# Hybrid encoder layer: the down projection product by product, gathered biases, values split once, a scheduler with a port shared by VectorE and GpSimd

## Chip, cores and metric

The kernel runs on one core of a Trainium2 chip. Its time is the device time of one execution in microseconds, the median of three runs. The core has a tensor engine (TensorE, PE in the profile; PEld are its weight loads), VectorE (DVE), ScalarE (ACT), GpSimd (POOL) and SyncE (SP), whose queue issues all DMAs here.

## The reference

One encoder layer of width 1024 on two sequences, p with 512 tokens and s with 1024, all in float32:

```python
mod = silu(c) @ w_ada + b_ada                       # sh1, sc1, g1, sh2, sc2, g2
n = rms_norm(x, ln1_g) * (1 + sc1) + sh1
q, k, v, xl, gl = split(n @ w_in)                   # 8 heads of 64; 512 columns for the recurrence
att = neighbourhood_attention(rms_norm(q), rms_norm(k), v, rpb)
xl = depthwise_conv(xl, 4 taps)
h = rg_lru(xl, forward) + rg_lru(xl, backward)
x = x + g1 * (concat([att, h * gelu(gl)]) @ w_out)
n2 = rms_norm(x, ln2_g) * (1 + sc2) + sh2
ug, uv = split(depthwise_conv(n2 @ w_up, 3 taps))   # 2816 each
x = x + g2 * ((gelu(ug) * uv) @ w_down)
```

Attention is on a grid 64 tokens wide: each token sees 8 rows by 16 columns around it, with a bias `rpb[head, row distance, column distance]` added to its scores before the softmax.

## The kernel before

**Precision.** Each float32 operand of a large product is split into a high part, rounded to TensorE's float32r, and a low part, the difference (`split`: a copy on ScalarE or VectorE, a subtraction on VectorE or GpSimd). A product is three matmuls: high by high, high by low, low by high (`mm3`).

**Strassen.** Feed-forward up and down are multiplied in Winograd's form of Strassen's scheme: seven products of half-size blocks in place of eight, with sums s1 to s4 of blocks of the left operand and t1 to t4 of the right one. The tuple `WINO` has their order, the PSUM bank in which each accumulates and whether it is the first there.

**Stages.** First the modulation and the first norm. Then the projections, attention and recurrence for four pairs of heads of p and four of s: the attention of one pair is recorded in turns with the projections of the next (`weave`). Then the output projection and the second norm, the up projection over 22 hidden tiles of 128 (four of them for p first, then the rest for both, then these four for s), with the convolution, GeLU and product done as tiles come, their results written to `g_d` in HBM. Last the down projection, from `g_d` and `w_down`.

**Down before (lines 1431 to 1534).** The 22 hidden tiles go in five chunks (`CHUNKS` = 2, 4, 6, 6 tiles, and the four of `ONLY_P`). In each chunk the loop goes over six pairs of token tiles; for each pair it loads four blocks of `g_d`, makes s1 to s4 and the parts of seven terms, and runs the seven products, each over the chunk's one to three pairs of hidden tiles. At the end of each product its bank is emptied: copies of products 1, 5 and 6, additions in the banks, and `add`, which takes the finished block into an accumulator in SBUF, or in the last chunk through the gate and the residual to the output. So every pair of token tiles is visited five times, and the banks are emptied in every visit. Terms of `w_down` are made once in a chunk (`wd_term`).

**Attention before (lines 1023 to 1105).** A query tile is 8 rows by 16 columns. Its bias is made on the chip for each head: a mask from HBM, turned to bfloat16 and kept for the sequence (`masks`), less a window of a table of the pair of heads, by an instruction on VectorE or GpSimd (line 1070). The scores have the wrong sign (the query's scale is -0.125), so that the softmax's maximum is a minimum. `qkv` writes the values to HBM in float32 (line 922 and 925); `values` loads them for each block of 16 query columns, 32 key columns wide, and splits them there (lines 1053 to 1055).

**Order.** The whole program is recorded and then put in order by a list scheduler (`run`, `_order`) that knows a cost for each instruction, the latest start that keeps TensorE going, and the memory. An instruction can have alternatives on another engine: `either=True` is ScalarE or VectorE, `pool=None` VectorE or GpSimd. `leave` decides whether the other engine would be done first, against this one's cost times a factor of the table `LEAN`. VectorE and GpSimd are planned as independent. Since one helper line emits all instructions, all have line L351 in the profile; tiles are named by the memory in which they lie (`arena_f`, `arena_r`, `piece0F`, ..., `bank` for PSUM). Two arenas divide 216 KiB a partition: F for plain data, R for parts of operands, with the share of R by stage in `STEPS` (`turn`).

Of the kernel before, what the change touches and what calls it, by code (L numbers as in the profile page):

```python
# [18 lines left out]
P = 128  # L19
D = 1024  # L20
KT = 8
# [6 lines left out]
TAB_R = 16  # L28
TAB_C = 48
# [9 lines left out]
LEAN = {("DVE", "POOL"): 0.389, ("DVE", "DVE"): 0.536, ("ACT", "ACT"): 0.611, ("ACT", "DVE"): 1.869, ("DVE", "ACT"): 1.004}  # L39
# from the end of one instruction to the start of one that waits for it  # L40
# [6 lines left out]
# products of Strassen's scheme in Winograd's form, in the order they run: name, terms of A and B, bank, first in its bank  # L47
# [3 lines left out]
CHUNKS = (2, 4, 6, 6)  # L51
# [4 lines left out]
class View:  # L56
    """A window of a buffer that has no address yet: the access pattern on a stand-in, and how to get it."""
# [32 lines left out]
    def span(self):  # L90
        """Partition range and byte range in the buffer that it can touch."""
# [43 lines left out]
class Piece:  # L135
    """Memory that belongs to one of two arenas at a time; plan holds (position in the program, arena) of each change."""
# [8 lines left out]
class Arena:  # L145
    """Memory in which buffers get their place when their first instruction is put in order."""
# [61 lines left out]
class Op:  # L208
    __slots__ = ("pos", "eng", "cost", "lat", "emit", "deps", "left", "users", "ready", "bufs", "aset", "start", "end", "vt", "done", "name", "alts", "all", "win", "ver", "key", "first", "move", "late", "strict")


class Recorder:
# [55 lines left out]
    def turn(self, step):  # L268
        """From here in the program the float32r arena has this much memory."""
# [6 lines left out]
    # buffers  # L276
# [21 lines left out]
    def pair(self, shape, name):  # L298
        """High and low parts of an operand; they get their places together."""
# [14 lines left out]
    # instructions  # L314
    def op(self, eng, cost, emit, reads, writes, aset=None, lat=0.0, also=(), alts=(), move=0.0):
# [3 lines left out]
        o.all = {eng: (cost, emit), **dict(alts)}  # L319
        o.first = eng  # L320
# [43 lines left out]
    def act(self, out, in_, func, scale=None, bias=None, accum_out=None, either=False):  # L364
# [8 lines left out]
        self.op("ACT", cost, self._emit(self.nc.scalar.activation, kw), [in_, scale, bias], [out, accum_out], aset=SETS.get(func), alts=alts)  # L373
# [8 lines left out]
    def vec(self, name, out, reads, per=1.045, base=67.0, alts=(), **kw):  # L382
# [4 lines left out]
        self.op("DVE", per * n + base + (60 if ps else 0), self._emit(getattr(self.nc.vector, name), kw), reads, w, alts=alts)  # L387
# [12 lines left out]
    def tt(self, out, in0, in1, op, pool=False):  # L400
        """On VectorE, on GpSimd (pool), or on whichever is free first (pool=None)."""
# [6 lines left out]
        else:  # L408
            self.op("DVE", *b, [in0, in1], [out], alts={"POOL": a} if pool is None else {})
# [4 lines left out]
    def mm(self, out, lhsT, rhs, start, stop, tile_position=None, also=(), cost=None, go_on=False):  # L414
        n = self._n(rhs)
        if cost is None:
            cost = max(64.0, n) / 2.4 + 2.5 if rhs.ap.dtype == F32R else max(214.0, n / 0.6)
# [6 lines left out]
        if start:  # L424
            # a group's first product clears the flags of the whole bank
# [13 lines left out]
    def mm3_rows(self, outs, sts, mvs):  # L439
        """outs[i] = sts[i].T @ mvs[i], each i on rows of the array of its own, side by side"""  # L440
# [15 lines left out]
    def mm2_rows(self, outs, sts, mvs):  # L456
        """outs[i] = sts[i][0].T @ mvs[i][0] + sts[i][1].T @ mvs[i][1], the second on rows of the array of its own"""
# [43 lines left out]
        # when each has to start for the tensor engine to go through the program without a halt  # L501
# [45 lines left out]
    def _order(self, occ):  # L547
        """The instructions and changes of memory in order, or where it halts and for which memory."""
# [20 lines left out]
        moved = 0.0  # L569
# [63 lines left out]
        while count < n:  # L633
# [69 lines left out]
            o.cost, emit = o.all[e]  # L703
            o.start, o.end = s, s + o.cost
# [38 lines left out]
def encoder(ctx: ExitStack, tc: tile.TileContext, x_p, x_s, c_t, ada, bada, lng, w_qkv, w_xg,  # L743
            qkg, tab, mask, lruv, gatew, w_out, w_up, w_down, ffv, y_p, y_s):
# [881 lines left out]
```

## Time and profile before

| | |
|---|---|
| median of three runs | 1893.22 us (1892.41 to 1893.79) |
| span of the profiled execution | 1892.9 us; its own time beside the span is not given, and the runs lie within 1 us of it |
| mean granted TensorE clock | 0.964 |
| TensorE busy | 1721.7 us, 91% |
| VectorE busy | 1495.2 us, 79% |
| ScalarE busy | 951.8 us, 50% |
| GpSimd busy | 838.9 us, 44% |
| moved by DMA | 201.12 MB, mean 106 GB/s |

Busy time is the time in which at least one instruction of the engine ran, waits inside an instruction included. Matmuls are pipelined and their ends modelled, so TensorE's share is read by stage and beside its clock. The granted clock has two levels, 1.2 and 2.4 GHz; 0.964 is their mean as a share of the upper one. Stages by time: modulation and start to 100 us; projections, attention and recurrence to 663; output projection to about 757; second norm and first up tiles to about 900; up to 1400, its end and the start of down to 1497; down to the end.

### The profile page before, as it was taken

The numbers are of one execution on the slowest core, as the hardware profiler recorded it, in microseconds if no ns is written. First come the engines' busy times: TensorE is split into PE (matmuls) and PEld (weight loads), VectorE is DVE, ScalarE is ACT, GpSimd is POOL, SyncE is SP. The second block draws the span as 40 slices with busy tenths as digits, with TensorE's granted clock in tenths as the row PEclk, the third lists the DMA queues.
The fourth block names the chain that finished last, engine by engine and source line by source line (L and its number), as shares of the span: only waits on it lengthen the run. The fifth ranks groups of instructions, "written<-read, shape, count | busy, mean of one in ns | idle before, by whom it ended". The sixth has DMA issues, their size and how long they took to land. (4 is left out here: it accounts for less than half of the span.)

```text
span 1892.9 us, 26075 instructions
## 1 busy us (share of the span) xinstructions
PE 1721.7 (91%) x8906; PEld 1416.1 (75%) x8906; DVE 1495.2 (79%) x2662; ACT 951.8 (50%) x1753; POOL 838.9 (44%) x656
## 2 busy tenths in 40 slices
PE   6987979989898899897999999999999888888978
PEld 3665767768687578797888888888887666776756
DVE  5697797897969874868767767667698998789998
ACT  3365863857676741454444444444454554243332
POOL 0364332362616321334333333333255776467874
PEclk9998989999999899998999999999999999999989
DMA  9435314040406465462122221221232331324322
GB/s 369 162 101 150 123 45 134 17 163 13 167 12 189 99 195 173 139 206 79 56 71 64 62 68 62 62 73 56 66 97 81 115 106 55 95 71 143 118 97 97
DMA packets 144695, 201.12 MB, mean 106 GB/s; under 512 B 15793, under 2 KB 83505, under 8 KB 144561
## 3 DMA queue, kind: packets, MB, share of 16 engines
q1 hardware_dynamic: 144560, 199.44, 33.2%
q8 instruction: 70, 1.15, 0.3%
q14 instruction: 65, 0.52, 0.1%
HBM read 157.97 MB, written 41.44 MB: 105 GB/s over the span
## 5 line engine op out<-in xcount | busy, mean ns | idle before, releaser
L351 PE MATMUL bank<-arena_r 128*128 128x512 f32 (+3 forms) x3487 | 859.6, 379 | 58.0 <-ACT piece0F L351 11.0
L351 PEld LDWEIGHTS bank<-arena_r 128*128 128x128 f32 (+1 forms) x3487 | 632.2, 192 | 192.3 <-issue 22.0
L351 PE MATMUL bank<-arena_r,piece0R 128*128 128x512 f32 (+3 forms) x1323 | 325.2, 346 | 8.5 <-DVE piece4F L351 4.4
L351 PEld LDWEIGHTS bank<-arena_r,piece0R 128*128 128x128 f32 (+1 forms) x1323 | 230.6, 194 | 41.5 <-issue 6.3
L351 POOL TENSOR_TENSOR arena_r<-arena_f,arena_r 128x256 fp32r<-128x256 f32 (+4 forms) x172 | 189.8, 1113 | 159.1 <-ACT arena_r L351 74.1
L351 POOL TENSOR_TENSOR arena_f<-arena_f 128x512 f32<-128x512 f32 (+5 forms) x149 | 178.9, 1207 | 99.6 <-issue 42.9
L351 ACT ACTIVATE arena_r<-arena_f 128x256 fp32r<-128x256 f32 (+4 forms) x245 | 115.0, 495 | 130.8 <-PE bank L351 77.8
L351 PE MATMUL bank<-arena_r,piece2R 128*128 128x512 f32 (+1 forms) x735 | 179.5, 335 | 0.0
L351 DVE SCALAR_TENSOR_TENSOR arena_f<-bank,arena_s,arena_f 128x255 f32<-128x255 f32 (+2 forms) x308 | 157.5, 535 | 21.2 <-ACT arena_f L351 10.5
L351 ACT ACTIVATE arena_f<-arena_f,arena_s 128x384 f32<-128x384 f32 (+2 forms) x166 | 101.7, 619 | 84.7 <-DVE arena_s L351 54.4
L351 PEld LDWEIGHTS bank<-arena_r,piece2R 128*128 128x128 f32 x735 | 126.6, 190 | 16.4 <-POOL piece2R L351 0.2
L351 PE MATMUL bank<-arena_r,piece4R 128*128 128x256 f32 (+1 forms) x453 | 137.5, 330 | 0.4 <-DVE arena_f L351 0.4
L351 DVE TENSOR_TENSOR arena_f<-arena_f 128x512 f32<-128x512 f32 (+5 forms) x148 | 134.8, 919 | 3.7 <-ACT arena_f L351 2.5
L351 DVE TENSOR_TENSOR arena_r<-arena_f,arena_r 128x256 fp32r<-128x256 f32 (+5 forms) x143 | 123.8, 882 | 6.6 <-ACT arena_r L351 2.6
L351 ACT ACTIVATE arena_f<-bank 128x512 f32<-128x512 f32 (+3 forms) x186 | 82.3, 454 | 75.1 <-DVE bank L351 36.9
L351 PE MATMUL bank<-piece0R,arena_r 128*128 128x512 f32 (+3 forms) x316 | 104.4, 398 | 2.1 <-DVE arena_s L351 2.0
L351 ACT ACTIVATE piece0R<-arena_f 128x512 fp32r<-128x512 f32 (+2 forms) x78 | 48.9, 627 | 113.1 <-PE bank L351 92.5
L351 ACT ACTIVATE arena_f<-bank,arena_s 128x512 f32<-128x512 f32 (+1 forms) x132 | 89.6, 683 | 24.5 <-PE bank L351 15.2
L351 DVE TENSOR_TENSOR bank<-bank,arena_f 128x512 f32<-128x512 f32 (+1 forms) x89 | 52.3, 589 | 51.3 <-PE bank L351 32.8
L351 PEld LDWEIGHTS bank<-arena_r,piece4R 128*128 128x128 f32 x453 | 83.5, 190 | 9.3 <-issue 0.8
L351 ACT ACTIVATE piece2R<-arena_f 128x512 fp32r<-128x512 f32 x63 | 39.8, 631 | 89.9 <-PE bank L351 77.9
L351 DVE SCALAR_TENSOR_TENSOR arena_f<-arena_f,arena_s 128x511 f32<-128x511 f32 (+3 forms) x102 | 70.9, 696 | 17.4 <-ACT arena_f L351 15.4
(432 smaller groups left out, 3214.1 us busy)
## 6 DMA issues: line engine op xcount, KB each, us to landing
arena_f<-in_w_up_dram SPq DMA_DIRECT2D x96, 256.0 KB
gd<-arena_f SPq DMA_DIRECT2D x62, 256.0 KB
piece2F<-in_ada_dram SPq DMA_DIRECT2D x18, 512.0 KB
arena_f<-in_w_qkv_dram SPq DMA_DIRECT2D x24, 384.0 KB
arena_f<-gd SPq DMA_DIRECT2D x39, 192.0 KB
piece3F<-in_ada_dram SPq DMA_DIRECT2D x14, 512.0 KB
arena_f<-gd SPq DMA_DIRECT2D x46, 128.0 KB
arena_f<-in_ada_dram SPq DMA_DIRECT2D x8, 512.0 KB
```

The source lines that it names most:

```text
L351: fn(**{k: (v.real() if isinstance(v, View) else v) for k, v in kw.items()})
```

## The change

**Down.** The loop is turned round: the seven products are outermost, then the eleven pairs of hidden tiles, then six tiles of 128 tokens. The left operand's halves are the first and the last 768 tokens. Each product accumulates in six banks over all eleven pairs; its blocks of `g_d` and `w_down` are loaded and its terms made and split for that product alone, s and t sums kept in SBUF between products where the next needs them. Then `product` takes the six banks to sums in SBUF or, by `done`, through gate and residual to the output. The last product goes over its tiles in three rounds (3, 2, 1), with the terms kept. The float32r arena has 64 KiB in down and 124 in the last product, in place of 112.

**Biases and values.** The host lays out the complete bias of every query tile and pair of heads (`bias_p`, `bias_s`, -1e30 outside the window), and attention loads it; masks, tables and the instruction between them go, and the query's scale is 0.125 with `scale=-1.0` in the reduction. The values are split when they leave PSUM in `qkv`, written as [high, low, low, high], 256 columns, and loaded as they are.

**Scheduler.** `LEAN` goes. Instructions on GpSimd, and on VectorE those with neither PSUM operand nor a form in `ONE_PORT`, hold a port: two of them are never planned at the same time. A float32r matmul costs n / 2.4 + 13.5 ns, at least 109, in place of n / 2.4 + 2.5. The comments go too.

```diff
-STEPS = (140, 134, 160, 176, 186, 112)
+STEPS = (140, 134, 160, 176, 186, 64, 124)
+ONE_PORT = ("tensor_reduce", "reciprocal")
+DOWN = (("1", "11", "11"), ("2", "12", "21"), ("5", "s1", "t1"), ("6", "s2", "t2"), ("7", "s3", "t3"), ("3", "s4", "22"), ("4", "22", "t4"))
+LAST = ((0, 1, 2), (3, 4), (5,))
...
+        o.port = {"POOL"} if eng == "POOL" or "POOL" in alts else set()
+        if port:
+            o.port.add("DVE")
...
-            cost = max(64.0, n) / 2.4 + 2.5 if rhs.ap.dtype == F32R else max(214.0, n / 0.6)
+            cost = max(max(64.0, n) / 2.4 + 13.5, 109.0) if rhs.ap.dtype == F32R else max(214.0, n / 0.6)
...
+            own = (max(s, port) if e in o.port else s) + o.alts[e][0]
...
-                    if max(clock[f], s) + ahead + cost < s + LEAN[o.first, e] * o.alts[e][0]:
+                    if max(clock[f], s, port if f in o.port else s) + ahead + cost < own:
...
+            if e in o.port:
+                s = max(s, port)
+                port = s + o.cost
...
-                vt = R.buf([P, 2, P], F32, "vt")
+                vt = R.buf([P, 2, 4, 64], F32R, "vt")
...
-                    R.copy(vt[:, u, :], pt[:, 256:384], either=True)
+                    v2 = pt[:, 256:384].rearrange("p (h d) -> p h d", h=2)
+                    R.act(vt[:, u, 0:4:3, :], v2, AF.Copy, either=True)
+                    R.tt(vt[:, u, 1:3, :], v2, vt[:, u, 0:4:3, :].bitcast(F32), ALU.subtract)
...
-            vr, vh = R.buf([P, nck, P], F32, "vr"), R.buf([P, nck, 2, 2, 64], F32R, "vh")
+            vh = R.buf([P, nck, 2 * P], F32R, "vh")
             for a in range(nck):
-                R.dma(vr[:, a, :], src[a, :, KB[cb]:KB[cb] + 32, :])
-            v4 = vr.rearrange("p a (h d) -> p a h d", h=2)
-            for hh in range(2):
-                R.act(vh[:, :, hh, hh, :], v4[:, :, hh, :], AF.Copy, either=True)
-                R.tt(vh[:, :, hh, 1 - hh, :], v4[:, :, hh, :], vh[:, :, hh, hh, :].bitcast(F32), ALU.subtract, pool=None)
+                R.dma(vh[:, a, :].bitcast(F32), src[a, :, KB[cb]:KB[cb] + 32, :])
...
+                bi = R.buf([P, 2, nk], F32, "bi")
+                R.dma(bi, {"p": bias_p, "s": bias_s}[q][j, var])
...
-                    bi = R.buf([P, nk], F32, "bi")
-                    R.tt(bi.rearrange("p (a b) -> p a b", b=32), msk[var].rearrange("p (a b) -> p a b", b=32), tbs[hh][:, a0:a0 + nr, b0:b0 + 32], ALU.subtract, pool=None)
...
+    nh, half = nt // 2, (TP + TS) // 2
+    pairs = list(range(ONLY_P // 2, NH // 2)) + list(range(ONLY_P // 2))
...
+    def block_a(k, z):
+        x = R.buf([P, half], F32, "gr")
+        h, r = 2 * k + int(z[1]) - 1, int(z[0]) - 1
+        R.dma(x, g_d[h, :, r * half:r * half + half])
+        return x
...
+    def term_a(name, k):
+        if name == "s1":
+            sa[k] = R.buf([P, half], F32, "s")
+            R.tt(sa[k], block_a(k, "21"), block_a(k, "22"), ALU.add, pool=None)
+        elif name == "s2":
+            R.tt(sa[k], sa[k], block_a(k, "11"), ALU.subtract, pool=None)
...
+            return halved(block_a(k, name), "g", None, [P, half])
+        return halved(sa[k], "g", None, [P, half])
...
+    def done(z, i, pt, x):
...
+        R.dma(x2, x2_d[q][row:row + P, cc])
+        R.tt(u, pt, x, ALU.add)
+        R.tt(u, u, g2[q][n], ALU.mult, pool=None)
+        R.tt(u, u, x2, ALU.add, pool=None)
+        R.dma(seqs[q]["y"][row:row + P, cc], u)
...
+        if name == "1":
+            x["1"] = R.buf([P, 512], F32, "x1")
+            R.act(x["1"], pt, AF.Copy, either=True)
+        elif name == "2":
+            done("11", i, pt, x["1"])
+        elif name == "5":
+            plus("15", "1")
+        elif name == "6":
+            plus("6", "1")
+            plus("156", "15")
+        elif name == "7":
+            plus("7", "6")
+            done("22", i, pt, x["156"])
+        elif name == "3":
+            done("12", i, pt, x["156"])
+        else:
+            done("21", i, pt, x["7"])
+
+    for name, ka, kb in DOWN:
+        last = name == DOWN[-1][0]
+        if last:
+            R.turn(6)
+        terms = {}
+        for tiles in LAST if last else (range(nh),):
+            pts = {i: R.bank("dn") for i in tiles}
+            for k in pairs:
+                if k not in terms:
+                    terms[k] = term_a(ka, k), term_b(kb, k)
+                (ah, al), w = terms[k]
+                for i in tiles:
+                    c = slice(i * P, i * P + P)
+                    R.mm3(pts[i], [(ah[:, c], al[:, c])], [w], start=k == pairs[0], stop=k == pairs[-1], go_on=True)
+            for i in tiles:
+                product(name, i, pts[i])
```

`plus(new, old)` adds a bank to an earlier sum into a new SBUF buffer; `block_b` and `term_b` do for `w_down` and t1 to t4 what `block_a` and `term_a` do for `g_d`.

## Rows read from the trace of the kernel before

**Rows 1.** The page's first part: busy time, share of the span, instructions.

```profile
PE 1721.7 (91%) x8906; PEld 1416.1 (75%) x8906; DVE 1495.2 (79%) x2662; ACT 951.8 (50%) x1753; POOL 838.9 (44%) x656
```

**Rows 2.** Windows by stage: length, busy us per engine (instructions), clock, DMA share, GB/s.

```profile
0.00:100.00 100.00, 81.17 (x382) 51.13 (x383) 61.65 (x163) 40.71 (x67) 25.47 (x31) 0.93 0.69 251
100.00:663.00 563.00, 496.29 (x2696) 398.51 (x2695) 474.61 (x1095) 372.94 (x705) 234.79 (x176) 0.95 0.33 102
663.00:757.00 94.00, 90.50 (x419) 75.05 (x418) 55.82 (x85) 30.57 (x49) 22.17 (x8) 0.98 0.56 185
757.00:900.00 143.00, 127.42 (x803) 114.89 (x802) 111.66 (x153) 71.38 (x117) 56.32 (x36) 0.94 0.45 140
900.00:1400.00 500.00, 498.80 (x2861) 439.66 (x2860) 353.54 (x576) 238.65 (x418) 180.27 (x125) 1.00 0.22 66
1400.00:1497.00 97.00, 87.55 (x368) 71.30 (x368) 85.89 (x156) 45.85 (x94) 58.65 (x65) 0.93 0.29 90
1497.00:1893.00 396.00, 339.93 (x1388) 265.54 (x1386) 352.07 (x440) 151.68 (x306) 261.25 (x217) 0.96 0.31 99
```

**Rows 3.** Timeline, TensorE, 1863 to 1888: start, length, instructions merged, idle before.

```profile
1863.12 23.88 PE L351 MATMUL bank<-arena_r 128*128 128x512 f32 x104 [0.44 <-ACT piece2F L351]
```

**Rows 4.** Waits of TensorE, 1497 to 1893: releaser, total us, times, longest.

```profile
PE bank L351 <- ACT piece0F L351: 11.0, 6, 3.9
PE bank L351 <- DVE bank L351: 10.5, 6, 2.2
```

**Rows 5.** Timeline, 1716 to 1724: single VectorE and GpSimd instructions.

```profile
1717.54 0.55 DVE L351 TENSOR_TENSOR arena_f<-arena_f 128x384 f32<-128x384 f32 x1
...
1717.81 1.44 POOL L351 TENSOR_TENSOR arena_r<-piece0F,arena_r 128x512 fp32r<-128x512 f32 x1 [0.74 <-PE bank L351]
1718.01 0.68 DVE L351 TENSOR_TENSOR piece3F<-bank,piece3F 128x512 f32<-128x512 f32 x1
...
1719.45 1.08 POOL L351 TENSOR_TENSOR arena_r<-arena_f,arena_r 128x384 fp32r<-128x384 f32 x1 [0.21 <-ACT arena_r L351]
1719.58 1.50 DVE L351 TENSOR_TENSOR piece3F<-piece3F,piece0F 128x512 f32<-128x512 f32 x1
...
1721.12 0.69 DVE L351 TENSOR_TENSOR piece3F<-piece3F,arena_f 128x512 f32<-128x512 f32 x1
```

**Rows 6.** Groups by shape, 1497 to 1893: busy us, mean ns, idle before.

```profile
L351 ACT ACTIVATE piece0F<-bank 128x512 f32<-128x512 f32 x34 | 20.2, 595 | 37.6 <-DVE bank L351 21.5 <-PE bank L351 9.5 <-DVE arena_f L351 2.7
...
L351 DVE TENSOR_TENSOR bank<-bank,piece0F 128x512 f32<-128x512 f32 x23 | 15.9, 690 | 1.8 <-PE bank L351 0.9 <-ACT piece0F L351 0.7
```

**Rows 7.** Groups by shape, whole span, 768 columns.

```profile
L351 ACT ACTIVATE arena_r<-arena_f 128x768 fp32r<-128x768 f32 x18 | 14.9, 840 | 6.1 <-DMA arena_f<-in_w_qkv_dram 6.0
...
L351 DVE TENSOR_TENSOR arena_r<-arena_f,arena_r 128x768 fp32r<-128x768 f32 x12 | 14.1, 1174 | 1.9 <-issue 1.7
```

**Rows 8.** Timeline, 1886 to 1893: the last products.

```profile
1885.71 1.29 PE L351 MATMUL bank<-arena_r 128*128 128x512 f32 x5
```

**Rows 9.** The page's DMA queues: packets, MB, share of 16 engines' span.

```profile
q1 hardware_dynamic: 144560, 199.44, 33.2%
```

**Rows 10.** Groups by shape, 100 to 757, with a bfloat16 operand.

```profile
L351 POOL TENSOR_TENSOR arena_f<-arena_f,piece3F 128x384 f32<-128x384 bf16 x8 | 10.0, 1269 | 3.1 <-PE bank L470 2.0 <-DMA vds<-arena_f 1.1
...
L351 DVE TENSOR_TENSOR arena_f<-arena_f 128x384 f32<-128x384 bf16 x8 | 6.5, 820 | 0.1
...
L351 DVE TENSOR_TENSOR arena_f<-arena_f,piece3F 128x384 f32<-128x384 bf16 x6 | 3.3, 544 | 0.0
```

**Rows 11.** Waits of TensorE, 100 to 663.

```profile
PE bank L351 <- DVE arena_r L351: 13.3, 11, 3.6
PE bank L470 <- issue: 8.5, 1, 8.5
PE bank L470 <- DVE arena_s L351: 8.4, 6, 1.8
PE bank L351 <- ACT piece2F L351: 7.2, 2, 5.2
```

More of the change, by code (lines that the diff above doesn't have):

```diff
@@ L208 @@
 class Op:
-    __slots__ = ("pos", "eng", "cost", "lat", "emit", "deps", "left", "users", "ready", "bufs", "aset", "start", "end", "vt", "done", "name", "alts", "all", "win", "ver", "key", "first", "move", "late", "strict")
+    __slots__ = ("pos", "eng", "cost", "lat", "emit", "deps", "left", "users", "ready", "bufs", "aset", "start", "end", "vt", "done", "name", "alts", "all", "win", "ver", "key", "first", "move", "late", "strict", "port")
 class Recorder:
@@ L312, in fixed_view, with op @@
         return self.dram(t, "fixed")
-    def op(self, eng, cost, emit, reads, writes, aset=None, lat=0.0, also=(), alts=(), move=0.0):
+    def op(self, eng, cost, emit, reads, writes, aset=None, lat=0.0, also=(), alts=(), move=0.0, port=False):
         o = Op()
@@ L372, in act @@
             alts["DVE"] = (1.045 * self._n(in_) + 127 if self._ps(in_) else 0.523 * self._n(in_) + 67, self._emit(self.nc.vector.tensor_copy, dict(out=out, in_=in_)))
-        self.op("ACT", cost, self._emit(self.nc.scalar.activation, kw), [in_, scale, bias], [out, accum_out], aset=SETS.get(func), alts=alts)
+        self.op("ACT", cost, self._emit(self.nc.scalar.activation, kw), [in_, scale, bias], [out, accum_out], aset=SETS.get(func), alts=alts, port=either and not self._ps(out, in_))
     def _act(self, out, in_, scale=None):
@@ L386, in vec @@
         w = [out] + ([kw["accum_out"]] if "accum_out" in kw else [])
-        self.op("DVE", per * n + base + (60 if ps else 0), self._emit(getattr(self.nc.vector, name), kw), reads, w, alts=alts)
+        self.op("DVE", per * n + base + (60 if ps else 0), self._emit(getattr(self.nc.vector, name), kw), reads, w, alts=alts, port=not ps and name not in ONE_PORT)
     def copy(self, out, in_, either=False):
@@ L408, in tt @@
         else:
-            self.op("DVE", *b, [in0, in1], [out], alts={"POOL": a} if pool is None else {})
+            self.op("DVE", *b, [in0, in1], [out], alts={"POOL": a} if pool is None else {}, port=not self._ps(out, in0, in1))
     def stt(self, out, in0, scalar, in1, op0, op1):
@@ L568, in _order @@
         aset = None
-        moved = 0.0
+        moved = port = 0.0
         tick = 0
@@ L790, in encoder @@
     g_d = scratch([NH, P, TP + TS], "gd")
-    v_d = {q: [scratch([s["T"], P], f"vd{q}{j}") for j in range(4)] for q, s in seqs.items()}
+    v_d = {q: [scratch([s["T"], 2 * P], f"vd{q}{j}") for j in range(4)] for q, s in seqs.items()}
     def rsqrt(ss, n, scale):
@@ L1021, in lru, with attend @@
         R.dma(cat_d[q][4 + c], h)
-    def masks(q):
-        nv, mcols, moff = (4, 256, 0) if q == "p" else (8, 384, 4 * 256)
-        out = []
-        for v in range(nv):
-            raw, m = R.buf([P, mcols], F32, "mkr"), R.buf([P, mcols], BF16, "msk")
-            R.dma(raw, mask[:, moff + v * mcols:moff + (v + 1) * mcols])
-            R.copy(m, raw)
-            out.append(m)
-        return out
-    def attend(q, msk, j, kqs):
+    def attend(q, j, kqs):
         kh, kl, qs = kqs
@@ new lines, in encoder, with block_b @@
+    g2 = {}
+    for q in seqs:
+        g2[q] = [R.buf([P, 512], F32, "g2b") for _ in range(2)]
+        for n in range(2):
+            R.dma(g2[q][n], g_dram[2][seqs[q]["i"]:seqs[q]["i"] + 1, n * 512:n * 512 + 512].broadcast_to([P, 512]))
+    def block_a(k, z):
[3 more added lines that the diff above has]
+        return x
+    def block_b(k, z):
+        x = R.buf([P, 512], F32, "wd")
+        h, n = 2 * k + int(z[0]) - 1, int(z[1]) - 1
+        R.dma(x, w_down[h * P:h * P + P, n * 512:n * 512 + 512])
+        return x
@@ new lines, in done @@
+    def done(z, i, pt, x):
+        m, n = int(z[0]) - 1, int(z[1]) - 1
+        t = m * nh + i
+        q = seq_of[t]
+        row, cc = t * P - off[q], slice(n * 512, n * 512 + 512)
+        x2, u = R.buf([P, 512], F32, "x2f"), R.buf([P, 512], F32, "u")
+        R.dma(x2, x2_d[q][row:row + P, cc])
[3 more added lines that the diff above has]
+        R.dma(seqs[q]["y"][row:row + P, cc], u)
+    sums = [{} for _ in range(nh)]
@@ new lines, in product, with plus @@
+    def product(name, i, pt):
+        x = sums[i]
+        def plus(new, old):
+            x[new] = R.buf([P, 512], F32, "x" + new)
+            R.tt(x[new], pt, x[old], ALU.add)
+        if name == "1":
[13 more added lines that the diff above has]
+            done("12", i, pt, x["156"])
+        else:
+            done("21", i, pt, x["7"])
@@ L1536, in encoder, with _places @@
     R.run()
-def _masks():
+def _places():
     import numpy as np
     out = []
-    for rows, halves, (kr0, knr) in ((8, 1, ((0,), (8,))), (16, 2, ((0, 4), (12, 12)))):
+    for rows, halves, knr in ((8, 1, 8), (16, 2, 12)):
         wr = min(8, rows)
+        at = np.full((halves, 4, 8, 16, knr, 32), 15 * 31, np.int64)
         for half in range(halves):
             for cb in range(4):
-                m = np.full((8, 16, knr[half], 32), BIG, np.float32)
                 for r in range(8):
-                    rs = min(max(half * 8 + r - wr // 2, 0), rows - wr)
+                    row = half * 8 + r
+                    rs = min(max(row - wr // 2, 0), rows - wr)
@@ L1556, in _layout @@
+        out.append(at.reshape(halves * 4, P, knr * 32))
+    return out
 def _layout(inp):
@@ L1595, in _layout @@
     return f
[L1598 removed]
+_ORDER = ["x_p", "x_s", "c_t", "ada", "bada", "lng", "w_qkv", "w_xg", "qkg", "bias_p", "bias_s", "lruv", "gatew",
           "w_out", "w_up", "w_down", "ffv"]
```

167 lines of the change are left out of this document (38 added, 129 removed).

## The prediction

> **What bounds the kernel now.** I read the busy shares first, then the windows by stage, then what the tensor engine waits for in the two loose stages, then how long single VectorE instructions take there. TensorE is busy 91% of the span, VectorE 79%, GpSimd 44% [rows 1]. TensorE's ends are modelled, so the stages tell more [rows 2]. From 900 to 1400 (feed-forward up) it is busy 498.8 of 500 us at clock 1.00: nothing can be won there. From 663 to 757 (output projection) it is busy 90.5 of 94 at 0.98: next to nothing. The start, 0 to 100, moves 251 GB/s with DMA at 0.69 and waits for the modulation weights; no edit touches it. What is loose: 100 to 663 (projections, attention, recurrence), 66.7 us idle and a clock of 0.95, which is 5% of 563 = 28 us more, 95 us lost; 757 to 900 (second norm, first up tiles), 15.6 idle and 6% of 143 = 8.6, 24 lost; 1400 to 1497, 9.5 and 7% of 97 = 6.8, 16 lost; and the down projection, 1497 to 1893.
>
> Down holds 1386 products of 512 columns (7 products x 6 token pairs x 11 pairs of hidden tiles x 3); the window shows 1388. Its last unbroken run has 104 of them in 23.88 us, 0.2296 each [rows 3], so 1386 need 318.2 us of the 396: 78 us are lost. They are lost to the engines that empty banks and make operands: TensorE's longest waits there are for ScalarE copies and for VectorE's additions in banks [rows 4], while VectorE is busy 352 of 396 us and GpSimd 261 [rows 2].
>
> Much of that busy time is blocking. At 1719.45 GpSimd starts a 1.08 us instruction; VectorE starts a 512-wide addition of two SBUF operands 0.13 us later and needs 1.50 us; the same kind takes 0.69 at 1721.12, with GpSimd idle. An addition that reads a bank takes 0.68 in the middle of a GpSimd instruction (1718.01) [rows 5]. So only VectorE work whose operands are all in SBUF is held up. The Trainium skill says the same more strictly (SBUF — State Buffer, Who interferes with whom): the port pair that the two share is an exclusive lock, and the loser waits for the whole of the other's instruction. By that rule GpSimd adds nothing beside VectorE's SBUF work; these rows agree, with 0.81 us of waiting, and the rule's own result is rival 2 below.
>
> **Down, product by product.** TensorE's work stays: 1386 products, 318.2 us. Emptying banks changes. Before, each of 30 visits (5 chunks x 6 pairs) empties its banks: from the code 162 additions or multiplications on a bank, 96 on SBUF, 108 copies. After, the sum over all 11 pairs stays in the bank: per tile 8 additions on a bank, 8 SBUF operations and one copy, for 6 tiles 48, 48 and 6. So 114 + 48 = 162 VectorE operations go, at 0.69 us (bank form mean 690 ns, [rows 6]; SBUF form 0.69 alone, [rows 5]) 112 us; and 102 ScalarE copies at 0.595, 61 us.
>
> Operand making stays in columns but comes in wider pieces: 7 splits of 768 and 7 of 512 columns for each of 11 pairs, and 4 sums of each. From 0.55 us at 384 and 0.69 at 512 [rows 5] the slope gives 0.97 at 768 (the row of that width averages 1.17 with blocking, [rows 7]). Low parts: 77 x (0.97 + 0.69) = 128 us; sums: 44 x 1.66 = 73; with the emptying, 96 x 0.69 = 66, VectorE would have 267 us of 318 if GpSimd did nothing: 84%. High parts on ScalarE: 77 x (0.840 + 0.595) = 110 us [rows 6, 7], 35%. So TensorE becomes the bound. Products 5, 6 and 7 are the tight ones: 11 x 3.3 = 36 us of terms and 4 to 8 of emptying in 45.5 us of TensorE each; products 1 and 2 need 18, but only some six pairs fit ahead (64 KiB over 10 KiB a pair). At a change of product the next one needs six banks of eight; a tile's last three products take 0.69 us and one bank read 0.69, two after products 6 and 7, so bank reuse about keeps pace. For the six changes I charge 1 us each (0 if all is emptied in time, 4 if a read queues behind two 768-wide splits), 4 for the start, 2 for clock dips. The tail stays: now 5.9 us from the last product's end (1885.71 + 1.29) to the end of the span [rows 8]; afterwards one bank addition, two SBUF ones and the same output DMA. Sum: 318.2 + 5.9 + 12 = 336 us instead of 396: **-60**. Bounds: 318 + 6 (-72) and, with VectorE's 352 us as they are plus the 12, 364 (-32).
>
> DMA grows. Blocks are loaded again for each product: 9 x 11 of 393 KB and 9 x 11 of 262 KB, with x2, the output and the gates 78.5 MB, against about 41. Products 5 and 7 load two of each per pair, 1.31 MB in 18 x 0.2296 = 4.13 us, 317 GB/s. The queue moved 199.44 MB in 33.2% of the 16 engines' 1892.9 us [rows 9], which is 317 GB/s at full share. So those two run at the edge, fed by what products 2 and 6 leave over (half the rate); over the stage it is 78.5 / 318 = 247 GB/s. I cost it at nothing, covered by that prefetch; without the cover, product 5 shares its 45 us with product 2's x2 and output (3.1 MB): 10 us.
>
> **Biases and values.** 96 operations that made a bias from mask and table go (64 of 384 columns, 32 of 256): 0.54 to 0.82 us at 384 columns on VectorE, 1.27 in the costliest group on GpSimd [rows 10], at the alone price 64 x 0.55 + 32 x 0.41 = 48 us of VectorE. Value splits go from 64 wider ones after loading to 48 of 128 columns at the bank: level on VectorE, some 20 us less on ScalarE. Added: 12.6 + 4.2 MB of biases less 8.4 MB of tables and masks, and values twice as wide (some 8 MB): 16 MB over 560 us, 29 GB/s on top of 102 [rows 2]; hidden, since they depend on no computation, or only on the earlier store. VectorE is busy 475 of 563 us in that stage, and of TensorE's waits the longest is for it, and the third (13.3 and 8.4 us, [rows 11]). A us off VectorE is worth between nothing and a us.
>
> **Scheduler.** It now plans GpSimd and VectorE's SBUF work as exclusive, and charges 0.227 us for a product where it charged 0.216, close to the 0.2296 measured. No instruction goes; the order and the split between engines change in the whole program. GpSimd's 235 us in 100 to 663 are some 110 us of VectorE at half the price; where they move, VectorE is no longer blocked. The trace can't price a new order: between -20 (of the order of the waits of [rows 11] coming back) and +50 us won. For the front, biases and order together, I take a third of the 95 lost: **-32** (bounds +15 and -80). The two loose stages round the up projection share only in the order: a sixth of 24 and a third of 16, **-4** and **-6** (bounds 0 and -25 together).
>
> Sum against the profiled execution's span: 1892.9 - 60 - 32 - 4 - 6 = 1790.9. The median of the runs is 1893.22, 0.3 above; predicted **1791 us**.
>
> **Rivals.**
> 1. *Down only* (0.20). The front is bound by chains (bank, softmax, transposes) and not by VectorE's load; it gives 5 and down 60: 1828. For it: in [rows 11] 8.5 us are a wait with no releaser and 7.2 are for ScalarE. Against: the two rows for VectorE come to 21.7.
> 2. *The lock stays* (0.08). GpSimd keeps a third of its 261 us in down, all of it blocking: 267 + 87 = 354, with the 12 and the tail 372, -24; front -10: 1859. For it: products 5 to 7 leave VectorE almost no slack, so the planner must give GpSimd something. Against: it can now place it under bank reads.
> 3. *Both stages reach TensorE* (0.08): down 324 (-72), front -80, others -25: 1716. Against: chains remain at the start of each head pair.
> 4. *Slower: DMA bounds down* (0.06). 78.5 MB through one queue issued in order. It decides below 78.5 / (396 + 42) = 179 GB/s, where the 42 us won elsewhere are eaten. After the start no window moves more than 185 GB/s [rows 2]; at the 140 of 757 to 900 the stage takes 561 us: 1893 + 165 - 42 = 2016. Against: that window has DMA at 0.45, so the queue was not full.
> 5. *The plan comes out as before* (0.01): within 0.2%.
>
> **How the numbers follow.** The forecast (1765 to 1815) has 0.55; 0.02 are left for an order that comes out otherwise for no nameable reason, half of it within 0.2%, half slower. 0.2%, 4 us, is about what a measurement of this kernel can tell from none. Faster 0.91 (forecast, 1, 2, 3), same 0.02, slower 0.07. The range of 1740 to 1850 holds the forecast, rival 1 and parts of 2 and 3.
>
> **What would show it.** Down: TensorE's busy share above 95% and clock at or near 1.00 from its first product to the end, in 325 to 350 us; bank-reading additions a third as many; DMA at 200 to 260 GB/s. 512-wide SBUF additions nearer 0.7 than 1.2 us, GpSimd well under 839 us. Front: no instruction on a bfloat16 operand, VectorE under 420 us in 563 or less. Wrong if down stays over 364 us, or if TensorE there waits for DMA, or if the front is not shorter though VectorE's load fell.

## The result, and the profile after

The changed kernel takes 1810.0 us (median of four runs, 1808.4 to 1811.9) where the kernel before takes 1893.5: 83.5 us less, a ratio of 0.9562 (95% interval 0.9548 to 0.9575). Forecast were 1791 us, with 1740 to 1850 as the range. The profiled execution took 1811.5 us, its span is 1809.5.

The page's busy times after, against [rows 1], and its DMA queue, against [rows 9]:

```profile
PE 1692.5 (94%) x8906; PEld 1408.4 (78%) x8906; DVE 1348.9 (75%) x2538; ACT 836.3 (46%) x1446; POOL 472.8 (26%) x298
```

```profile
q1 hardware_dynamic: 133328, 252.27, 42.0%
```

GpSimd works 473 us instead of 839, VectorE 1349 instead of 1495. The queue moves 52.8 MB more; 37.5 was the estimate for down alone and 16 for the front.

The windows by stage, against [rows 2]. Their bounds are the times at which TensorE has done as much of its work as at the bounds of before:

```profile
0.00:90.00 90.00, 76.27 (x384) 49.42 (x384) 55.44 (x160) 38.57 (x59) 11.87 (x14) 0.98 0.75 276
90.00:628.00 538.00, 489.15 (x2699) 399.21 (x2699) 423.62 (x1074) 377.71 (x696) 89.14 (x58) 0.94 0.43 140
628.00:719.00 91.00, 88.91 (x411) 73.19 (x410) 54.43 (x88) 26.83 (x48) 2.40 (x1) 1.00 0.57 191
719.00:850.00 131.00, 125.94 (x801) 113.91 (x800) 108.72 (x151) 70.80 (x117) 55.84 (x36) 0.97 0.48 153
850.00:1357.00 507.00, 502.43 (x2865) 441.24 (x2864) 375.44 (x698) 204.15 (x353) 89.17 (x65) 1.00 0.21 65
1357.00:1441.00 84.00, 83.05 (x370) 67.82 (x369) 65.47 (x102) 40.28 (x65) 26.79 (x18) 1.00 0.32 102
1441.00:1809.50 368.50, 326.73 (x1388) 263.64 (x1386) 265.75 (x271) 77.98 (x113) 197.61 (x108) 0.95 0.59 203
```

| stage | before, us | after, us | won | forecast |
|---|---|---|---|---|
| start | 100 | 90 | 10 | 0 |
| projections, attention, recurrence | 563 | 538 | 25 | 32 |
| output projection | 94 | 91 | 3 | 0 |
| second norm, first up tiles | 143 | 131 | 12 | 4 |
| up | 500 | 507 | -7 | 0 |
| end of up | 97 | 84 | 13 | 6 |
| down | 396 | 368.5 | 27.5 | 60 |

The bounds are rounded to the us. All stages but down gave some 56 us where 42 were forecast; down gave less than half of its term. In the front no instruction with a bfloat16 operand is left (against [rows 10]), and TensorE's longest waits there are now for ScalarE (against [rows 11]):

```profile
PE bank L355 <- ACT piece3F L355: 13.9, 2, 12.7
PE bank L474 <- ACT piece4F L355: 6.8, 8, 2.4
PE bank L474 <- DVE arena_s L355: 5.2, 4, 2.9
...
PE bank L355 <- DVE arena_r L355: 3.0, 4, 1.5
```

What TensorE waits for in down (releaser, total us, times, longest), against [rows 4]: no longer copies from banks and additions in them, but low parts of operands, which VectorE and GpSimd make.

```profile
PE bank L355 <- DVE arena_r L355: 21.6, 8, 18.8
PE bank L355 <- POOL arena_r L355: 9.7, 2, 5.0
PE bank L355 <- ACT arena_r L355: 3.3, 4, 0.9
```

The longest wait is at the start of product 3 (shown below); the two for GpSimd are early in product 5 and in product 4 (timeline):

```profile
1542.29 5.95 PE L355 MATMUL bank<-arena_r 128*128 128x512 f32 x17 [4.98 <-POOL arena_r L355]
...
1756.49 10.17 PE L355 MATMUL bank<-arena_r 128*128 128x512 f32 x34 [4.74 <-POOL arena_r L355]
```

All three come right behind products 2, 7 and 3, at whose end `done` takes finished blocks through the gate and the residual: 12 operations on SBUF each time.

The same stage cut at the changes of product (order 1, 2, 5, 6, 7, 3, 4; columns as in [rows 2]: length, busy TensorE, weight loads, VectorE, ScalarE, GpSimd, clock, DMA share, GB/s):

```profile
1441.20:1486.10 44.90, 44.90 (x200) 37.17 (x199) 27.52 (x47) 11.87 (x19) 3.35 (x2) 1.00 0.85 287
1486.10:1532.40 46.30, 45.61 (x199) 36.92 (x198) 34.66 (x32) 12.21 (x18) 27.65 (x16) 1.00 0.93 329
1532.40:1584.60 52.20, 47.22 (x200) 38.37 (x200) 42.58 (x30) 13.13 (x19) 47.45 (x26) 0.93 0.58 197
1584.60:1629.40 44.80, 44.80 (x199) 37.12 (x198) 33.33 (x26) 14.06 (x20) 38.98 (x22) 1.00 0.69 232
1629.40:1676.00 46.60, 45.24 (x200) 37.11 (x200) 42.17 (x33) 17.44 (x27) 45.77 (x25) 1.00 0.82 271
1676.00:1751.10 75.10, 50.91 (x200) 38.31 (x198) 51.16 (x61) 8.22 (x11) 25.54 (x16) 0.86 0.40 134
1751.10:1809.50 58.40, 47.84 (x199) 38.45 (x198) 34.14 (x47) 0.85 (x1) 8.86 (x6) 0.94 0.15 54
```

Four of the seven products run in 44.8 to 46.6 us, at or near TensorE's pace. Product 5 (third row) takes 52, product 3 (sixth) 75, product 4 with the tail (seventh) 58. In product 3 the granted clock falls to its lower level in the stall, at 1683, and stays there until 1703, into the run behind it, whose first seven products take 3.53 us, 0.50 each in place of 0.227. The tail is as forecast: the last product starts its last run at 1801.03 and ends at 1803.91, and one bank addition and two operations on SBUF later the output goes, 5.6 us in all (5.9 before, [rows 8]).

```profile
1801.03 2.88 PE L355 MATMUL bank<-arena_r,piece0R 128*128 128x512 f32 x12
...
1805.40 0.69 DVE L355 TENSOR_TENSOR piece2F<-piece2F,piece1F 128x512 f32<-128x512 f32 x1
```

Around the stall of 18.8 us at the start of product 3 the two vector engines look like this (timeline of after; start, length, operation, and in brackets TensorE's idle time and its releaser):

```profile
1665.33 2.04 DVE L355 TENSOR_TENSOR piece0F<-arena_f,piece0F 128x768 f32<-128x768 f32 x1
1666.52 2.00 POOL L355 TENSOR_TENSOR arena_r<-piece0F,arena_r 128x512 fp32r<-128x512 f32 x1
1667.30 2.04 DVE L355 TENSOR_TENSOR piece0F<-piece0F 128x768 f32<-128x768 f32 x1
...
1668.48 2.00 POOL L355 TENSOR_TENSOR arena_r<-piece4F,arena_r 128x512 fp32r<-128x512 f32 x1
...
1669.26 2.04 DVE L355 TENSOR_TENSOR arena_r<-piece3F,arena_r 128x768 fp32r<-128x768 f32 x1
...
1674.94 1.29 POOL L355 TENSOR_TENSOR piece0F<-piece0F,arena_f 128x512 f32<-128x512 f32 x1
...
1676.19 1.29 POOL L355 TENSOR_TENSOR piece3F<-piece3F,arena_f 128x512 f32<-128x512 f32 x1
...
1685.28 1.74 DVE L355 TENSOR_TENSOR piece3F<-piece3F,piece4F 128x512 f32<-128x512 f32 x1
1686.43 2.25 POOL L355 TENSOR_TENSOR arena_f<-piece0F,arena_f 128x768 f32<-128x768 f32 x1
1686.94 2.28 DVE L355 TENSOR_TENSOR piece5F<-piece5F,piece1F 128x512 f32<-128x512 f32 x1
...
1688.64 1.70 POOL L355 TENSOR_TENSOR arena_r<-piece2F,arena_r 128x512 fp32r<-128x512 f32 x1
...
1694.69 2.01 DVE L355 TENSOR_TENSOR arena_r<-arena_f,arena_r 128x768 fp32r<-128x768 f32 x1
...
1696.76 3.53 PE L355 MATMUL bank<-arena_r 128*128 128x512 f32 x7 [18.80 <-DVE arena_r L355]
```

From 1665 to 1669 VectorE's 768-wide operations and GpSimd's 512-wide ones take turns: one of each in 1.96 us (1665.33 to 1667.30). VectorE alone takes 0.96 and 0.69 for the same two (measured in `down_vector` below; the slope in the prediction gave 0.97). From 1685 on VectorE's 512-wide gate operations take 1.7 to 2.3 us in place of 0.69, each beside a GpSimd instruction, and the 768-wide low part for which TensorE waits comes behind them, at 1694.69.

### The profile page after: what moved, and what is told of

Read it like the earlier page. It is cut to its first block, busy times and chain, and to the rows that moved or that the text cites. A ratio compares the mean times of both kernels' runs of the same rounds, so it can differ in the third digit from the quotient of the medians.

```text
span 1809.5 us, 24917 instructions
## 1 busy us (share of the span) xinstructions
PE 1692.5 (94%) x8906; PEld 1408.4 (78%) x8906; DVE 1348.9 (75%) x2538; ACT 836.3 (46%) x1446; POOL 472.8 (26%) x298
## 4 chain that ended last, share of the span: by engine, by line
PE 70%; DVE 8%; ACT 4%; issue 3%; DMA 3%; POOL 1%; SPq 0%; DVEq 0%; ACTq 0%; POOLq 0%
PE bank L355 68%; DVE arena_f L355 2%; PE bank L474 2%; DVE arena_r L355 1%; ACT arena_f L355 1%; DVE piece3F L355 1%; DVE piece5F L355 1%; DVE piece0F L355 1%; DVE piece4F L355 1%; ACT L355 1%; ACT piece4F L355 1%; DVE piece0R L355 1%; DMA piece4F<-in_x_s_dram 1%; ACT piece5F L355 1%; DVE arena_s L355 1%
## 5 line engine op out<-in xcount | busy, mean ns | idle before, releaser
L355 PE MATMUL bank<-arena_r 128*128 128x512 f32 (+2 forms) x1882 | 449.6, 376 | 39.4 <-DVE arena_r L355 24.9
L355 PEld LDWEIGHTS bank<-arena_r 128*128 128x128 f32 (+1 forms) x1882 | 340.6, 193 | 114.8 <-DVE arena_r L355 31.7
L355 PE MATMUL bank<-arena_r,piece0R 128*128 128x384 f32 (+2 forms) x1895 | 407.1, 332 | 2.9 <-DVE piece0R L355 1.1
L355 PEld LDWEIGHTS bank<-arena_r,piece0R 128*128 128x128 f32 x1895 | 318.7, 191 | 30.0 <-issue 9.1
L355 PE MATMUL bank<-piece0R,arena_r 128*128 128x512 f32 (+1 forms) x980 | 281.1, 397 | 0.0
L355 PEld LDWEIGHTS bank<-piece0R,arena_r 128*128 128x128 f32 (+1 forms) x980 | 180.4, 189 | 44.6 <-issue 5.4
L355 PE MATMUL bank<-piece0R 128*128 128x512 f32 (+3 forms) x708 | 201.1, 389 | 2.3 <-ACT piece3F L355 1.2
L355 DVE SCALAR_TENSOR_TENSOR arena_f<-bank,arena_s,arena_f 128x511 f32<-128x511 f32 (+1 forms) x310 | 159.9, 538 | 23.6 <-ACT arena_f L355 15.9
L355 ACT ACTIVATE arena_f<-arena_f,arena_s 128x384 f32<-128x384 f32 (+3 forms) x185 | 112.0, 617 | 95.0 <-DVE arena_f L355 70.6
L355 PEld LDWEIGHTS bank<-piece0R 128*128 128x128 f32 (+1 forms) x708 | 122.4, 191 | 31.5 <-issue 4.9
```

Of the source, the lines that this page charges most:

```text
L355: fn(**{k: (v.real() if isinstance(v, View) else v) for k, v in kw.items()})
```

## The experiments

Each was timed with the kernel before on the same chip; ratios are to that, with their 95% intervals. Each expectation sets two or three theories against each other.

### The parts alone: bias_only, sched_only, down_only, and the new work under the old planner

`bias_only` and `down_only` carry one part of the diff each, under the planner of before; `sched_only` carries the planner alone; `after_nosched` is the changed kernel with the planner of before. The edits are the parts of the diff shown above; that of `sched_only`, for one:

```diff
+        o.port = {"POOL"} if eng == "POOL" or "POOL" in alts else set()
...
-            cost = max(64.0, n) / 2.4 + 2.5 if rhs.ap.dtype == F32R else ...
+            cost = max(max(64.0, n) / 2.4 + 13.5, 109.0) if rhs.ap.dtype == F32R else ...
...
-                    if max(clock[f], s) + ahead + cost < s + LEAN[o.first, e] * o.alts[e][0]:
+                    if max(clock[f], s, port if f in o.port else s) + ahead + cost < own:
```

> The kernel before with one part of the change: biases from the host and values split once; planner and down projection as before. Of the 83.5 us won, some 36 were won by the time the front (projections, attention, recurrence) is through, 20 round the up projection, 28 in down. Theory A, the parts add up and the front's gain is mostly VectorE work removed: 1868 to 1875 us (18 to 25 won), all of it before the output projection. Theory B, the front's gain is the new planner's, and removed VectorE work is worth little to a chain-bound stage: 1885 to 1893.

Measured: 1909.5 us, ratio 1.0084 (1.0061 to 1.0107): 16 us slower. Neither theory had that. TensorE is some 6 us ahead of the kernel before at 280 us, and behind only after 630; between the same points of its work the front takes 588 us for 563. This is the timeline there: SyncE's issue of DMAs, then the first instruction that ScalarE could do, then TensorE's.

```profile
612.68 14.88 SPq L351 DMA_DIRECT2D gd<-arena_s  x2
...
627.65 11.81 SPq L351 DMA_DIRECT2D arena_r<-vds  x5
...
639.56 2.27 SPq L351 DMA_DIRECT2D piece2F<-in_w_out_dram  x3
...
649.24 1.06 ACT L351 ACTIVATE piece0R<-piece2F 128x1024 fp32r<-128x1024 f32 x1 [17.41 <-DMA piece2F<-in_w_out_dram]
...
653.05 0.90 PE L470 MATMUL bank<-ident,arena_f 128*128 128x128 f32 x3 [19.55 <-ACT piece2F L351]
```

The queue is held for 14.9 us while it issues two writes of gate vectors and for 11.8 us over five loads of values; the weights of the output projection go out behind them, and ScalarE, whose next instruction is their split, stands for 17.4 us. TensorE then waits 19.55 us for it, most of the 25 us that the front is longer. The removed work did not become time; the order of one queue cost more than it gave. The changed kernel still has a wait of this kind, the 12.7 us for ScalarE shown above.

> The kernel before with only the planner changed: VectorE's SBUF work and GpSimd exclusive, no table of factors, 0.227 us for a 512-column product. No instruction goes. Theory A: 1865 to 1880 us, half of it round the up projection. Theory B: 1845 to 1860, with GpSimd's busy time down by a third or more in every stage.

Measured: 1847.7 us, ratio 0.9752 (0.9735 to 0.9769): 47 us won, theory B's size. By stage: 10 at the start, some 10 in the front, 12 in second norm and first up tiles, 12 at the end of up, 4 in down, 2 in the output projection; up loses 6, as in the changed kernel. GpSimd's total falls from 839 to 718 us only, so B's reason is half right: in the front it still works 206 us (235 before), but VectorE is busy 437 us for 475:

```profile
90.00:643.00 553.00, 494.11 (x2689) 396.53 (x2688) 437.20 (x1037) 395.09 (x755) 206.44 (x190) 0.95 0.34 106
```

> The kernel before with only the new down projection, under the old planner. Theory A, the removed emptying of banks is worth what it costs: 1855 to 1870 us, down in 360 to 370. Theory B, without the port in its plan the old planner puts a third of the wide operand work on GpSimd beside VectorE, and both block each other: 1880 or slower, with 768-wide VectorE operations near 2 us on average.

Measured: 1878.6 us, ratio 0.9908 (0.9889 to 0.9927): 16 won, near B. Down takes 380 us, with 67 in product 5 and 63 in product 3. GpSimd does 41 of the 119 operations of 768 columns, a third as in B, but VectorE's average 1.5 us and not 2.

> The changed kernel with the old planner (factors, no port, 0.216 us a product). Theory A, parts add up: the sum of the gains of biases alone and down alone, 1835 to 1850 us. Theory B, planner and new work need each other: 1860 or more.

Measured: 1880.0 us, ratio 0.9924 (0.9906 to 0.9942), theory B: 15 won, where the two parts alone sum to about none. So the parts do not add up: planner 47, down 16, biases -16 alone make 47, all together 83.5. Under the new planner the rest is worth 36; under the old one 15.

### The planner's two halves: port_only, pe_only

```diff
 # port_only: of the planner's change, without
-            cost = max(max(64.0, n) / 2.4 + 13.5, 109.0) if rhs.ap.dtype == F32R else ...
+            cost = max(64.0, n) / 2.4 + 2.5 if rhs.ap.dtype == F32R else ...
 # pe_only: of the planner's change, that line alone
```

> The kernel before with one half of the planner's change: VectorE's SBUF work and GpSimd exclusive, factors gone, a product still charged 0.216 us. The whole planner alone won 47 us. Theory L (the lock in the plan is what counts): 1845 to 1860 us, GpSimd's busy time near 720 us as with the whole. Theory T (TensorE's true price is what counts, since due times are counted in it): 1875 to 1895.

> The other half alone: a product charged 0.227 us, the factors and the independent engines as before. Theory L: 1880 to 1895 us. Theory T: 1845 to 1865. If each half gives a part and they add up to 47: some 1865 to 1875 here and the rest in the other.

Measured: port alone 1858.5 us, 0.9814 (0.9799 to 0.9829), 35 won; price alone 1906.3, 1.0068 (1.0053 to 1.0083), 13 lost. Theory L holds for the first; the second is slower than either theory had it. The true price of a product pays only with the rest: 12 more on top (0.9752 against 0.9814, intervals apart). `port_only` makes two edits at once, though: it plans the two engines as exclusive, and the table `LEAN` goes. No run takes the table away alone, so that the exclusive plan by itself is what pays is likely and not shown. The 6 to 7 us lost in up come only with both halves: between the same points of TensorE's work up takes 506 us in `sched_only`, 499 in `port_only` and in `pe_only`, 500 before; why is open.

### The biases under the new planner: after_nobias

> The changed kernel with masks, tables and values as before. Biases alone were 16 us slower under the old planner, almost all of it one 20 us stall before the transposes of the last pair of heads, where ScalarE stands at a weight load that is late in SyncE's queue. Theory S (an accident of that order): here the biases are worth the VectorE work that they take away, so without them 1825 to 1840 us. Theory C (the stage is bound by chains, the work removed is worth nothing): 1805 to 1815.

Measured: 1815.2 us, 0.9583 (0.9567 to 0.9599), beside 0.9562 (0.9548 to 0.9575) of the changed kernel: the intervals touch, so biases and values are worth some 4 us of the total, hardly told from none. By stage the front has 17 us less with them (538 against 556 between the same points of TensorE's work, rounded) and down 11 us more (368 against 357, 75 against 65 in product 3). Theory S fits the front, theory C the total. Stages move by their order and placement alone too: `down_room` below records the same program up to down as the changed kernel, and its front takes 5 us more, its output projection 6, and its down starts 15 us later. So the 17 us are not shown to be all the biases'.

### The missing time in down: down_vector, down_room, down_both, down_nogate, nosched_room

```diff
 # down_vector
-            R.tt(sa[k], block_a(k, "21"), block_a(k, "22"), ALU.add, pool=None)
+            R.tt(sa[k], block_a(k, "21"), block_a(k, "22"), ALU.add, pool=False)
 ... and so in all sums, low parts and gate operations of down
 # down_room
-STEPS = (140, 134, 160, 176, 186, 64, 124)
+STEPS = (140, 134, 160, 176, 186, 90, 124)
 # down_both: both. down_nogate: without
-        R.tt(u, u, g2[q][n], ALU.mult, pool=None)
-        R.tt(u, u, x2, ALU.add, pool=None)
```

> The changed kernel with no GpSimd in down: each sum, low part and gate operation there is VectorE's. Down took 368 us where 336 were forecast; TensorE stalls 19 us at the change from product 7 to product 3, 5 us each early in product 5 and in product 4, and some 7 us in small waits in product 3. Theory P (the lock): in products 7 and 3 GpSimd and VectorE run SBUF work back to back and each waits for the other's; without GpSimd the same work takes VectorE half the time, and the stalls shrink: 1785 to 1797 us. Theory R (room): the parts have 64 KiB, six pairs ahead, which a burst of emptying uses up; GpSimd helps then, and without it it is the same or slower: 1808 to 1825. Theory D (DMA at 0.87 to 0.95 of its share in products 1, 2 and 7): no change, 1805 to 1815.

Measured: 1808.9 us, 0.955 (0.9531 to 0.9568): no change, down 365. The loss moves (product 5 takes 56 us, product 3 60), theory P falls; 1808.9 lies within the ranges of both R and D, and the next run decides between them. Its window and one group of low parts, in the changed kernel and here, hold a finding:

```profile
1443.00:1808.50 365.50, 329.46 (x1390) 263.84 (x1389) 268.12 (x398) 65.79 (x91) 0.00 (x0) 0.97 0.61 204
```

```profile
L355 DVE TENSOR_TENSOR arena_r<-piece0F,arena_r 128x768 fp32r<-128x768 f32 x20 | 31.3, 1582 | 10.6 <-ACT arena_r L355 7.6 <-POOL arena_r L355 3.0
...
L355 DVE TENSOR_TENSOR arena_r<-piece0F,arena_r 128x768 fp32r<-128x768 f32 x20 | 19.0, 956 | 6.2 <-ACT arena_r L355 3.4 <-PE bank L355 2.5
```

VectorE is busy 268 us with all the work, 398 instructions, and was busy 266 with 271 while GpSimd did 108 others in 198 us (some 20 more came to it from ScalarE, which has 91 for 113). What GpSimd took over, VectorE spent waiting for it: GpSimd's 67 operations of 512 columns and 41 of 768 are some 85 us at VectorE's own 0.69 and 0.96, and VectorE's 98 and 76 of these widths took some 80 us more in the changed kernel than at that price.

> The changed kernel with 90 KiB in place of 64 for operand parts in products 1 to 3 of the order's first six, so 26 KiB less for blocks and sums. Theory R: nine pairs ahead ride over the burst, 1780 to 1795 us. Theory P: the two engines still block each other; 1800 to 1810. Theory D: less room for blocks on their way, 1815 or more.

Measured: 1782.9 us, 0.9413 (0.9387 to 0.9439): theory R. The windows by product:

```profile
1456.20:1501.10 44.90, 44.90 (x199) 37.08 (x198) 33.11 (x51) 13.92 (x21) 2.86 (x2) 1.00 0.84 285
1501.10:1546.10 45.00, 45.00 (x200) 37.04 (x198) 40.72 (x44) 11.50 (x17) 14.99 (x10) 1.00 0.95 339
1546.10:1591.10 45.00, 45.00 (x200) 37.15 (x200) 41.28 (x29) 12.04 (x16) 40.80 (x21) 1.00 0.61 221
1591.10:1636.00 44.90, 44.90 (x200) 37.20 (x199) 42.62 (x27) 14.27 (x21) 42.52 (x24) 1.00 0.61 195
1636.00:1685.00 49.00, 47.04 (x199) 38.14 (x198) 38.08 (x35) 19.15 (x28) 42.37 (x22) 0.97 0.87 293
1685.00:1731.80 46.80, 45.30 (x200) 37.13 (x199) 43.52 (x35) 15.00 (x21) 46.48 (x25) 1.00 0.67 222
1731.80:1782.10 50.30, 44.99 (x199) 36.93 (x197) 32.12 (x35) 3.31 (x6) 18.92 (x12) 0.97 0.17 63
```

Six products run in 47 us or less (the last row has the tail in it), one in 49, and down takes 326 us. The 90 KiB stand until the last product, which has 124 in both. The work is the same; it is done earlier: VectorE is busy 33 and 41 us in the two light products where it had 28 and 35, and product 3 no longer starts with nothing ready. Theory D falls too: with less room for blocks, product 2 moves 339 GB/s at a share of 0.95 and none of TensorE's waits that the trace shows there is for a DMA.

The edit reaches beyond down: the numbers in `STEPS` are also the borders of the pieces into which memory is divided (`KIB_R = sorted(set(STEPS))`), so the whole program is placed and ordered anew. Each of the three versions with 90 KiB reaches down later than the same version with 64: 15 us here, 13 in `down_both`, 16 in `nosched_room`. So the 42 us won in down are 27 in all; no run tells whether the later start is a price of the room or only another order.

> Both: no GpSimd in down and 90 KiB for parts. If P and R each hold a part of the 32 us missing: 1770 to 1785 us, down 330 to 340. If only one does: the better of the two alone.

Measured: 1781.6 us, 0.9408 (0.9391 to 0.9425), down 323: the better of the two alone. This and `down_room` are the fastest versions with the whole output, 28 and 27 us below the changed kernel; the intervals do not tell them apart.

```profile
1457.00:1780.00 323.00, 314.65 (x1386) 259.66 (x1384) 262.77 (x395) 66.18 (x92) 0.00 (x0) 1.00 0.66 228
```

> The changed kernel without the gate's multiplication and the residual's addition at the end of down (the output lacks both): 48 SBUF operations of 512 columns less, the loads of x2 and the writes of the output stay. Theory P, taken as load on VectorE and GpSimd at the change from product 7 to 3: the 19 us stall goes and the wait early in product 5 shrinks, 1775 to 1790 us. Theory D: the stalls stay, 1800 or more.

Measured: 1774.1 us, 0.9367 (0.9347 to 0.9387), down 324: a us below the range of theory P in the sense of load. With 64 KiB and GpSimd the stall is gone as well, since the burst is smaller: it takes the burst and the short lead together to make it.

```profile
1446.00:1770.20 324.20, 316.69 (x1386) 258.99 (x1384) 230.55 (x228) 78.37 (x114) 173.99 (x95) 1.00 0.65 224
```

> The changed kernel with the old planner and 90 KiB for parts in down. Down took 372 us under the old planner with 64 KiB, 368 under the new one, 326 under the new one with 90. If room alone bounds down: 330 to 340 us for it here, 1838 to 1850 in all. If it takes both, the port in the plan and the room: 360 or more, 1865 to 1880.

Measured: 1873.4 us, 0.9891 (0.9874 to 0.9908). Down takes 352.5 us, some 20 less than under the old planner with 64 KiB, and 26 more than under the new one with 90; the total hides most of it, as the stages ahead of down are 16 us longer. So room is worth 20 under the old planner and 42 under the new, and the answer lies between the two that were offered.

```profile
1519.00:1871.50 352.50, 322.38 (x1387) 264.07 (x1385) 269.84 (x270) 77.39 (x110) 178.86 (x99) 0.97 0.61 205
```

## Why the prediction was right, and where it was not

**The total.** 1810.0 us lies in the forecast's span of 1765 to 1815, and that is partly luck: 32 us were missing in down, and 14 more than forecast came from the other stages. By its own sign, "Wrong if down stays over 364 us", the account of down was wrong: 368.5. There TensorE is busy 89% and not over 95%, at a clock of 0.95, and the 98 operations of 512 columns that VectorE does on SBUF average 1.12 us, nearer 1.2 than 0.7. The other signs came out: VectorE's additions and multiplications on banks 48 for 162 in the traces, DMA at 203 GB/s, GpSimd at 473 us, no bfloat16 operand in the front, and VectorE there at 424 us, 4 over the limit named.

**What bounded the kernel.** Right for up, where nothing was won (7 us were lost), and the output projection, 3 us. At the start 10 us were won where none was forecast, since no edit touched it; `sched_only` has them too, so they are the new order's.

**Down: the engines' work.** TensorE needed 44.9 us for a product of 198, 314 us in all (318 in the sum). VectorE's 267 us, if GpSimd did nothing, are the 268 and 263 measured in `down_vector` and `down_both`. DMA was hidden, as forecast: none of TensorE's waits is for it. But the product at the edge was 2, with 329 GB/s at a share of 0.93, about twice what its own blocks need (7.2 MB in 46 us); products 5 and 7 moved 197 and 271. The full rate, by estimate, lies above the 317 GB/s that the prediction took from [rows 9]: 329 at 0.93 makes some 354. The tail: 5.6 for 5.9.

**Down: the step that failed** is "For the six changes I charge 1 us each ..., 4 for the start, 2 for clock dips", 12 us. In place of that the seven products cost 48 us over TensorE's pace: 30 in product 3, 8 in product 4, 7 in product 5. Some 36 of them are waits, and in some 12 TensorE works longer for the same products, for the most part in those three, where the clock is at 0.86, 0.94 and 0.93. The prediction had both causes on the page, products 5 to 7 at 40 to 44 us of VectorE in 45.5, and "only some six pairs fit ahead", but put a price on neither. By its sum these three products leave VectorE little slack, so the parts made ahead have to last through the bursts behind products 2 and 7; six pairs did not. `down_room` and `down_nogate` show it from both sides: with more made ahead, or a smaller burst, down takes 326 and 324 us, below the 336 of the sum.

**Front and loose stages.** 25 us for 32 in the front, 25 for 10 in the two stages round up. The front's size is about right, but its term was a third of what was lost there, taken for biases and order together, without a price for either. The runs give the biases at most 17 us of it under the new planner and a loss under the old. The planner alone gives 47 us in the whole kernel, some 10 of them in the front; since the parts do not add up, the 25 cannot be shared out.

**Rivals.** Down only (1): no, the front gained. The lock stays (2): it does stay, VectorE's 266 us with GpSimd are the proof, but it costs nothing net: without GpSimd down takes 365 us for 368, and with 90 KiB 323 for 326. That its 372 us for down are near the 368 measured is chance: it had VectorE busy 354 us, GpSimd's share on top of VectorE's own 267. Both stages reach TensorE (3): not here, but down does so with 90 KiB. DMA bound (4): no, 329 GB/s in product 2 and no wait for it, against the 179 from which it decides.

## What to carry to other kernels

A plan that lists two engines as parallel when they take turns gives away time everywhere at once: here that constraint, with the table of factors gone, was worth 35 us alone, and both edits of the work under the old planner 15. An average load of 84% hides three products that the prediction's own sum puts at 88 to 97%: for each burst ask how far ahead the engines that make operands can run, and what memory limits that. And when an order is made anew for the whole program, compare stage by stage: stages whose recorded work is the same moved by 5 or 6 us each between versions, 15 in sum ahead of down, as much as some of the edits under test.

## What the runs showed of the hardware that was not expected

Two vector engines on SBUF operands did less than one: a 768-wide operation on VectorE and a 512-wide one on GpSimd take 1.96 us together, in turns, and 0.96 and 0.69, 1.65 in sum, on VectorE alone. The Trainium skill (SBUF — State Buffer, Who interferes with whom) has the loser wait for the whole of the other's instruction. Here it waits for nearly the whole: alone and one behind the other, the 768-wide operations start 0.87 us apart on VectorE (`down_vector`) and the 512-wide ones 1.25 on GpSimd (1674.94 and 1676.19 in the timeline above, while VectorE reads banks), 2.12 us for one of each against the 1.96 measured in turns, and the measurement decides. DMA kept 329 to 339 GB/s over 45 us with rows of 2 and 3 KB, at a share of 0.93 to 0.95.
